# Feed-forwards' first products: 18 of 22 chunk pairs by seven half-size products each

## The chip, the cores and the metric

The kernel runs on one core of a Trainium2 chip, as one program. The metric is device microseconds (us) from its start to its end, the median of the runs shown. TensorE (PE in the profile) multiplies matrices out of SBUF into PSUM; VectorE (DVE), ScalarE (ACT) and GpSimd (POOL) work beside it on elementwise instructions, each in its own order; SyncE's queue (SP) issues most of the weight loads.

## The reference, cut to what matters

Two transformer blocks run one after the other over 512 tokens of 1024 features, in float32. Each has a gated feed-forward ahead of its token mixer and another behind it, four in all (f1, f2 in block 1, f3, f4 in block 2). Each feed-forward is

```python
DFF = 2816
u = rms_norm(x, gain)                 # (512, 1024)
a, b = jnp.split(u @ w_in, 2, axis=-1)   # w_in (1024, 5632): a the gate, b the up half
x = x + 0.5 * ((jax.nn.silu(a) * b) @ w_out)   # block 1 norms the product once more
```

The change touches `u @ w_in`, in all four places, and nothing of the mathematics behind it.

## The kernel before

Everything is held feature-major: a tile has 128 features on the partitions and the 512 tokens along it. A float32 product is made of three float32r products (`mm3`, L258 to L261): high part by high part, then the activations' low part, then the weights' low part. A weight piece is loaded as 128 x 8 x 128 floats (512 KB) into one of three `raw` buffers; ACT writes its high part (L247) and DVE the difference, its low part (L248). `lin` (L284) makes one chunk of 128 output features: 8 steps of the contraction by 3 products, 24 matmuls of 512 columns.

`ffn` (L449) goes through 22 pairs of chunks, one of the gate and one of the up half. For each pair it makes the two products (48 matmuls), multiplies both by the per-token factor R (L463 and L464, out of PSUM into SBUF on DVE), takes Silu on ACT (L94), multiplies (L466) and splits the result into high and low (L310 on ACT, L311 on DVE) for the second product with `w_out`, which follows when all 22 are there (tiles f1o, f2o, f3o, f4o). The norm's factor R comes late: the unnormalised input `g x` is split first (tiles u0 to u7), and in f1, f2 and f3 the first four chunks (pairs 0 and 1) are made ahead by `lin_ahead` (L295) in halves of 256 tokens while the stage before it still ends. f4 has nothing made ahead. Six PSUM banks of 512 columns hold chunk products at one time (NF = 6), two more the rest.

A scheduler of the language sets each engine's order of instructions from the order of the code, by its own estimate of times, and the buffers by their pools' counts. In f1, the constants of the mixers (`late_constants`, some 30 small DVE instructions, L152 to L232 and L546 to L548) are made at pair 2. Tiles of all feed-forwards lose their digits in the trace: f_3g_p is chunk 3 of the gate in whichever feed-forward the time says.

Of the kernel before, what the change touches and what calls it, by code (L numbers as in the profile page):

```python
# [18 lines left out]
P = 128  # L19
T = 512  # L20
# [8 lines left out]
FIRST = (0, DFF, P, DFF + P)  # L29
NM = 4  # L30
# [6 lines left out]
# block 1: 0-3 a step of an HGRN head, 4-7 of an mLSTM head; '.' of the products, in the order ORDER1; a-d an HGRN  # L37
# head's forget gate, e-h the silu of a convolution, A-H an output gate, w-z two gated heads; P the feed-forward's banks
# [3 lines left out]
# block 2: 0-7 a step of a stick-breaking head, a-h of a latent head; '.' and ',' of the products, in the orders ORDER2X  # L42
# and ORDER2Y; s a branch gate, q and k the scales of the latent heads
# [7 lines left out]
def block_kernel(ctx, tc, I, out):  # L51
# [3 lines left out]
    act = ctx.enter_context(tc.tile_pool(name="act", bufs=72))  # L55
    wraw = ctx.enter_context(tc.tile_pool(name="wraw", bufs=3))
# [5 lines left out]
    def psum_pools(**spec):  # L62
        """The PSUM banks shared out anew, by what they hold."""
        if "stack" in banks:
            banks["stack"].close()
        st = banks["stack"] = ExitStack()
        banks["nm"] = spec["m"]
        for tag, n in spec.items():
            banks[tag] = st.enter_context(tc.tile_pool(name="ps" + tag, bufs=n, space=PSUM, reuse_waits="tile"))
# [12 lines left out]
    def table(name):  # L82
        """The activations from here on, in this order to those before, use one table set."""
        ld = S.preload_act_table_set(name).ins  # L84
        for i in group["ins"]:
            tc.add_manual_dep(ld, i, after, reason="table")
        group["load"], group["ins"], group["name"] = ld.name, [], name
# [10 lines left out]
    def in_turn(prev, i):  # L98
        """Keeps an engine's instruction i behind the instruction named prev; the name of i."""
        if prev is not None:  # L100
            tc.add_manual_dep(i.ins, prev, after, reason="turn")
        return i.ins.name
# [74 lines left out]
    def late_constants():  # L177
# [33 lines left out]
        # the rotation's tables (cos and sin by the head norms' gains)  # L211
# [46 lines left out]
    def mm3(o, w, u, first, last):  # L258
        M.matmul(o, w[0], u[0], start=first, stop=False)  # L259
        M.matmul(o, w[0], u[1], start=False, stop=False)  # L260
        issued["last"] = M.matmul(o, w[1], u[0], start=False, stop=last).ins.name  # L261
# [3 lines left out]
    def lin_narrow(raw, n, us, R, name):  # L265
        """The product with n columns (held raw) times R, the high and low parts of the weights side by side."""
        ws = whi.tile([P, KD, 2 * n], F32R, tag="hi", name=name + "_h")
        S.activation(ws[:, :, 0:n], raw, AF.Copy)
        V.tensor_tensor(ws[:, :, n:], raw, ws[:, :, 0:n].bitcast(F32), ALU.subtract)
        o = ps(name + "_p")  # L270
        for k in range(KD):
            wide = lambda: M.matmul(o[0:2 * n, :], ws[:, k, :], us[k][0], start=k == 0, stop=k == KD - 1)
            if k == 0:
                wide()
            M.matmul(o[0:n, :], ws[:, k, 0:n], us[k][1], start=False, stop=False)
            if k > 0:
                wide()
        a, b = (A(f"{name}_{i}", shape=(n, T)) for i in range(2))
        V.tensor_tensor(a, o[0:n, :], R[0:n, :], ALU.mult)
        V.tensor_tensor(b, o[n:2 * n, :], R[n:2 * n, :], ALU.mult)  # L280
        V.tensor_tensor(a, a, b, ALU.add)
        return a

    def lin(w, c0, us, name):  # L284
        """A 128-column chunk of us^T w, feature-major."""
        if (w.tensor.name, c0) in issued:
            return issued.pop((w.tensor.name, c0))
        n = len(us)
# [30 lines left out]
    def rsqrt_newton(v, n, name):  # L319
        """1 / sqrt(v) without the activations' tables."""  # L320
# [17 lines left out]
    def token_rs(parts, n, name, blocks=range(NT), o=None, behind=None):  # L338
        """1 / sqrt(sum / n + eps) of the tokens: a square root and a step of Newton's."""
# [20 lines left out]
    class Squares:  # L360
        """The sum of the squares of the n chunks of features, as tiles to be summed over the partitions."""
# [16 lines left out]
    class Normed:  # L378
        """The parts of g x, chunk by chunk as x comes, and the per-token factor r."""
# [70 lines left out]
    def ffn(x, nx, w_in, w_out, post, nxt, ahead, name):  # L450
# [4 lines left out]
        hs = []  # L455
        for m in range(KF):
            if m == 2 and name == "f1":
                late_constants()
            n = f"{name}_{m}"
            pg = lin(w_in, m * P, us, n + "g")  # L460
            pu = lin(w_in, DFF + m * P, us, n + "u")
            gr, ur = A(n + "gr"), A(n + "ur")
            V.tensor_tensor(gr, pg, R, ALU.mult)  # L463
            V.tensor_tensor(ur, pu, R, ALU.mult)  # L464
            lut(gr, gr, AF.Silu)
            V.tensor_tensor(ur, gr, ur, ALU.mult)  # L466
            hs.append(split(ur, n + "h"))
# [11 lines left out]
    def lin_tok(w, us, c0, ncol, name, done, group=NT, bank=ps):  # L479
        """Products with the tokens on the partitions, group blocks of tokens at a time; done(t, o) takes a block's."""  # L480
# [30 lines left out]
    class Fillers:  # L511
        """Named generators, run one after the other a step at a time."""
# [17 lines left out]
    def causal_av(pd, pa, pb, v, o):  # L530
        """o[vdim, t] = sum_s v[s] p[s, t] over the blocks (diagonal, rows 0 and 2, row 1)."""
# [7 lines left out]
    def mixer1(x, nx, nxt, ahead):  # L539
# [191 lines left out]
        def mlstm_factor(hs):  # L731
            """1 / max(|den|, exp(-m)) times the head norm's factor, for the heads hs."""
# [105 lines left out]
        def head(c):  # L838
            """The next step of head c (0 to 3: HGRN, 4 to 7: mLSTM)."""
# [40 lines left out]
    def mixer2(x, nx, nxt):  # L880
# [6 lines left out]
        def sb_qk(j):  # L887
            """The queries or keys of two heads, their exact parts stacked: (high, high) against (high, low)."""
# [40 lines left out]
        def sb(h):  # L929
# [31 lines left out]
            # the parts, and those of the sums over the key blocks that follow (in place)  # L961
# [27 lines left out]
        # MLA latents  # L989
# [26 lines left out]
        def rope(src, j, t, nh, name):  # L1016
            """src (P, nh, 32), with the norm's gains of q (j=0) or k (j=1), rotated: a + b."""
# [24 lines left out]
        # queries and keys of the heads, token-major  # L1042
# [317 lines left out]
```

## Time and profile before

| what | value |
|---|---|
| runs | 2267.64, 2268.68, 2275.91 us; median 2268.68 us |
| profiled execution | its span, from the first to the last instruction, is 2267.5 us; what lies around the span is not in the trace, and the nearest run is 0.1 us above it |
| granted TensorE clock, mean | 0.993 |
| PE busy | 2247.1 us (99%) |
| DVE busy | 1151.6 us (51%) |
| ACT busy | 881.5 us (39%) |
| POOL busy | 119.6 us (5%) |

The engines work beside each other, so that their busy times don't add up. PE's busy time counts from the start of a matmul to its modelled end, and it says that PE had something in flight, not that it ran at its best rate.

### The profile page before, as it was taken

What the parts mean: (1) busy time and instruction counts of PE and PEld (TensorE: products, weight loads), DVE (VectorE), ACT (ScalarE), POOL (GpSimd) and SP (SyncE); (2) the same over time, 40 slices, a digit from 0 to 9 for tenths busy, and PEclk for the clock granted to TensorE, in tenths of its full rate; (3) what the DMA queues carried; (4) which work ended last, traced back from release to release, by engine and by line L of the source; (5) the groups of instructions that cost most, each with busy time, mean ns of one, the idle gap of its engine ahead of it and who ended that gap; (6) DMA issues with size and microseconds to landing.
All of it is one profiled execution on the core that took longest, in us unless ns stands there. A gap on an engine that the chain in (4) does not pass through costs nothing.

```text
span 2267.5 us, 27653 instructions
## 1 busy us (share of the span) xinstructions
PE 2247.1 (99%) x11074; PEld 1870.9 (83%) x11074; DVE 1151.6 (51%) x1938; ACT 881.5 (39%) x1344; POOL 119.6 (5%) x156
## 2 busy tenths in 40 slices
PE   8999999999999999999999999999999999999999
PEld 7888888888788888889888888877778888888887
DVE  5644323778648444325644433476674654444334
ACT  4323223556635333223432322566654442233222
POOL 3000001000112000001000001000000010000000
PEclk9999999999889999999999999999999999999999
DMA  5333333322112333332333333321131233333331
GB/s 151 93 96 100 95 94 91 88 62 75 38 47 85 102 93 102 93 96 73 112 93 101 89 96 104 85 66 48 46 89 34 79 112 94 102 93 96 96 107 65
DMA packets 364836, 197.22 MB, mean 87 GB/s; under 512 B 10007, under 2 KB 356516, under 8 KB 364708
## 3 DMA queue, kind: packets, MB, share of 16 engines
q1 hardware_dynamic: 364100, 195.37, 30.0%
q8 instruction: 87, 1.43, 0.3%
q0 software_dynamic: 608, 0.09, 0.0%
q14 instruction: 41, 0.34, 0.0%
HBM read 193.33 MB, written 2.10 MB: 86 GB/s over the span
## 4 chain that ended last, share of the span: by engine, by line
PE 98%; DVE 1%; ACT 0%; DMA 0%; issue 0%; SPq 0%; DVEq 0%
PE f1o_p L260 2%; PE f2o_p L259 2%; PE f2o_p L260 2%; PE f1o_p L259 2%; PE f2o_p L261 2%; PE f1o_p L261 2%; PE f4o_p L259 2%; PE f3o_p L261 2%; PE f4o_p L261 2%; PE f3o_p L259 2%; PE f3o_p L260 2%; PE f4o_p L260 2%; PE gt_p L260 1%; PE gt_p L259 1%; PE gt_p L261 1%; PE f_p L260 1%
## 5 line engine op out<-in xcount | busy, mean ns | idle before, releaser
L248 DVE TENSOR_TENSOR f1o_l<-f1o_r,f1o_h 128x1024 fp32r<-128x1024 f32 (+1 forms) x24 | 27.3, 1136 | 76.6 <-ACT f1o_h L247 76.6
L248 DVE TENSOR_TENSOR f2o_l<-f2o_r,f2o_h 128x1024 fp32r<-128x1024 f32 (+1 forms) x24 | 27.3, 1136 | 76.6 <-ACT f2o_h L247 76.6
L247 ACT ACTIVATE f2o_h<-f2o_r 128x1024 fp32r<-128x1024 f32 (+1 forms) x24 | 23.8, 990 | 85.7 <-PE f2o_p L260 73.0
L247 ACT ACTIVATE f1o_h<-f1o_r 128x1024 fp32r<-128x1024 f32 (+1 forms) x24 | 23.8, 990 | 85.7 <-PE f1o_p L260 68.4
L247 ACT ACTIVATE f3o_h<-f3o_r 128x1024 fp32r<-128x1024 f32 (+1 forms) x24 | 23.8, 990 | 85.3 <-PE f3o_p L260 53.2
L247 ACT ACTIVATE f4o_h<-f4o_r 128x1024 fp32r<-128x1024 f32 (+1 forms) x24 | 23.8, 990 | 85.0 <-PE f4o_p L260 52.8
L376 POOL TENSOR_TENSOR f_acc<-f_acc,f_sq 128x256 f32<-128x256 f32 (+1 forms) x42 | 38.9, 927 | 316.9 <-ACT f_sq L375 299.5
L248 DVE TENSOR_TENSOR f3o_l<-f3o_r,f3o_h 128x1024 fp32r<-128x1024 f32 (+1 forms) x24 | 27.3, 1136 | 54.0 <-ACT f3o_h L247 54.0
L248 DVE TENSOR_TENSOR f4o_l<-f4o_r,f4o_h 128x1024 fp32r<-128x1024 f32 (+1 forms) x24 | 27.3, 1135 | 52.5 <-ACT f4o_h L247 52.5
L84 ACT ACT_TABLE_LOAD x36 | 46.2, 1283 | 1.4 <-PEq L1341 0.8
L376 POOL TENSOR_TENSOR m_acc<-m_acc,m_sq 128x256 f32<-128x256 f32 (+1 forms) x18 | 20.1, 1115 | 348.8 <-ACT m_sq L375 348.8
L260 PE MATMUL m1o_p<-mix_l,m1o_h 128*128 128x256 f32 (+1 forms) x88 | 29.3, 334 | 0.0
L261 PE MATMUL m1o_p<-mix_h,m1o_l 128*128 128x256 f32 (+1 forms) x88 | 29.2, 334 | 0.0
L259 PE MATMUL m1o_p<-mix_h,m1o_h 128*128 128x256 f32 (+1 forms) x88 | 28.6, 336 | 0.0
L376 POOL TENSOR_TENSOR pl_acc<-pl_acc,pl_sq 128x512 f32<-128x512 f32 x6 | 10.3, 1710 | 341.6 <-ACT pl_sq L375 341.6
L248 DVE TENSOR_TENSOR gt_l<-gt_r,gt_h 128x1024 fp32r<-128x1024 f32 x16 | 19.6, 1224 | 12.9 <-ACT gt_h L247 12.6
L94 ACT ACTIVATE l<-l 128x384 f32<-128x384 f32 (+1 forms) x48 | 24.2, 554 | 3.1 <-DVE l L949 3.0
L247 ACT ACTIVATE pg_h<-pg_r 128x1024 fp32r<-128x1024 f32 x8 | 8.5, 1061 | 42.6 <-PE pp L496 19.4
L94 ACT ACTIVATE e<-ms,mx,sck 128x512 f32<-128x512 f32 (+3 forms) x32 | 19.5, 614 | 14.0 <-DVE mx L1135 13.8
L260 PE MATMUL wo_p<-mg_l,wo_h 128*128 128x512 f32 x64 | 24.8, 390 | 0.0
L259 PE MATMUL wo_p<-mg_h,wo_h 128*128 128x512 f32 x64 | 24.8, 389 | 0.0
L376 POOL TENSOR_TENSOR f2p_acc<-f2p_acc,f2p_sq 128x512 f32<-128x512 f32 x6 | 7.7, 1288 | 322.9 <-ACT f2p_sq L375 322.9
(4287 smaller groups left out, 7533.5 us busy)
## 6 DMA issues: line engine op xcount, KB each, us to landing
f1o_r<-in_ffn_w_out_dram SPq DMA_DIRECT2D x16, 512.0 KB, 3.8
f2o_r<-in_ffn_w_out_dram SPq DMA_DIRECT2D x16, 512.0 KB, 4.3
f3o_r<-in_ffn_w_out_dram SPq DMA_DIRECT2D x16, 512.0 KB, 4.3
gt_r<-in_w_in_dram SPq DMA_DIRECT2D x16, 512.0 KB, 4.0
f4o_r<-in_ffn_w_out_dram SPq DMA_DIRECT2D x16, 512.0 KB, 4.1
f_r<-in_ffn_w_in_dram SPq DMA_DIRECT2D x12, 512.0 KB, 5.0
mg_r<-in_w_mix_in_dram SPq DMA_DIRECT2D x8, 512.0 KB, 4.0
m1o_r<-in_w_mix_out_dram SPq DMA_DIRECT2D x8, 512.0 KB, 4.2
```

Of the source, the lines that this page charges most:

```text
L84: ld = S.preload_act_table_set(name).ins
L94: i = S.activation(out, in_, func, **kw).ins
L247: S.activation(hi, raw, AF.Copy)
L248: V.tensor_tensor(lo, raw, hi.bitcast(F32), ALU.subtract)
L259: M.matmul(o, w[0], u[0], start=first, stop=False)
L260: M.matmul(o, w[0], u[1], start=False, stop=False)
L261: issued["last"] = M.matmul(o, w[1], u[0], start=False, stop=last).ins.name
L376: G.tensor_tensor(acc[:, sl], acc[:, sl], q[:, sl], ALU.add)
```

## The change

Pairs 4 to 21 of each feed-forward (18 of 22) are made in another way. Gate chunk, up chunk, the two halves of the 1024 features and the two halves of the 512 tokens make a 2 x 2 by 2 x 2 block product, and Strassen's scheme (in Winograd's form) makes it of seven block products in place of eight, with sums and differences of the blocks ahead and behind. A block product here has 4 steps of the contraction by 3 products: 12 matmuls of 256 columns; seven of them are 84. Two of them share an accumulator, so that four regions of 256 columns (`ab`, `cd`, two banks) hold a pair.

`strassen_input` runs once per feed-forward: it makes the normalised input `un = g x R` (8 DVE instructions of 512 columns), 16 differences of 256 columns on POOL, and 28 forms of 256 columns, each split into a high part (ACT) and a low part (DVE). Evictions of pairs 0 and 1 are written between its parts. `strassen_pair` loads the two weight chunks (`r0`, `r1`), makes four sums of 512 columns on POOL, and splits four weight matrices a, b, c and d (1024, 512, 1024 and 1024 columns; in before two of 1024). Its evictions are two ACT copies and five DVE instructions of 256 columns that read PSUM (and mostly one SBUF tile). The steps of a pair and of the next are written interleaved. The splits of all 22 results stand behind the last pair, `late_constants` at pair 6. There are 70 activation buffers for 72, and 4 raw buffers for 3. Comments and docstrings went too. The core of the diff:

```diff
+NDIRECT = 4
+HT = T // 2
+HK = KD // 2
...
-    act = ctx.enter_context(tc.tile_pool(name="act", bufs=72))
-    wraw = ctx.enter_context(tc.tile_pool(name="wraw", bufs=3))
+    act = ctx.enter_context(tc.tile_pool(name="act", bufs=70))
+    wraw = ctx.enter_context(tc.tile_pool(name="wraw", bufs=4))
...
+    def strassen_input(x, nx, R, between):
+        un, forms = [None] * KD, [{} for _ in range(HK)]
+        def normed(k):
+            un[k] = A(f"{nx.name}_n{k}")
+            V.scalar_tensor_tensor(un[k], x[k], nx.g(k), R, ALU.mult, ALU.mult)
+        def form(k, name, src, sign=1.0):
+            t = A(f"{nx.name}_{name}{k}", F32R)
+            hi, lo = t[:, 0:HT], t[:, HT:]
+            S.activation(hi, src, AF.Copy, scale=sign)
+            if sign > 0:
+                V.tensor_tensor(lo, src, hi.bitcast(F32), ALU.subtract)
+            else:
+                V.scalar_tensor_tensor(lo, src, sign, hi.bitcast(F32), ALU.mult, ALU.subtract)
+            forms[k][name] = hi, lo
+        for k in range(HK):
+            normed(k)
+            form(k, "b11", un[k][:, 0:HT])
+        between(0)
+        for k in range(HK):
+            normed(HK + k)
+            form(k, "b21", un[HK + k][:, 0:HT])
+        between(1)
+        d1, d2 = [], []
+        for k in range(HK):
+            b11, b12, b22 = un[k][:, 0:HT], un[k][:, HT:], un[HK + k][:, HT:]
+            d1.append(A(f"{nx.name}_d1{k}"))
+            G.tensor_tensor(d1[k][:, 0:HT], b12, b11, ALU.subtract)
+            G.tensor_tensor(d1[k][:, HT:], b22, b12, ALU.subtract)
+            form(k, "n1", d1[k][:, 0:HT], -1.0)
+        for k in range(HK):
+            form(k, "t3", d1[k][:, HT:])
+        for k in range(HK):
+            b21, b22 = un[HK + k][:, 0:HT], un[HK + k][:, HT:]
+            d2.append(A(f"{nx.name}_d2{k}"))
+            G.tensor_tensor(d2[k][:, 0:HT], b22, d1[k][:, 0:HT], ALU.subtract)
+            G.tensor_tensor(d2[k][:, HT:], d2[k][:, 0:HT], b21, ALU.subtract)
+            form(k, "t2", d2[k][:, 0:HT], -1.0)
+        for k in range(HK):
+            form(k, "b22", un[HK + k][:, HT:])
+            form(k, "t4", d2[k][:, HT:])
+        return forms
+    def strassen_pair(w, c0, c1, forms, name, done):
+        r0, r1 = (wraw.tile([P, KD, P], F32, tag="raw", name=f"{name}_r{i}") for i in range(2))
+        for r, c in ((r0, c0), (r1, c1)):
+            nc.sync.dma_start(out=r, in_=w[:, c:c + P].rearrange("(k p) c -> p k c", p=P))
+        def parts(r, nm, n=KD):
+            if n == KD:
+                hi, lo = whi.tile([P, n, P], F32R, tag="hi", name=nm + "_h"), wlo.tile([P, n, P], F32R, tag="lo",
+                                                                                     name=nm + "_l")
+            else:
+                hi, lo = (act.tile([P, n, P], F32R, tag="a", name=f"{nm}_{j}") for j in "hl")
+            S.activation(hi, r, AF.Copy)
+            V.tensor_tensor(lo, r, hi.bitcast(F32), ALU.subtract)
+            return [(hi[:, k, :], lo[:, k, :]) for k in range(n)]
+        first, last = slice(0, HK), slice(HK, KD)
+        g1 = parts(r0, name + "a")
+        s1 = act.tile([P, HK, P], F32, tag="a", name=name + "_s1")
+        G.tensor_tensor(s1, r1[:, first], r1[:, last], ALU.add)
+        g2 = parts(s1, name + "b", HK)
+        G.tensor_tensor(r1[:, first], r0[:, first], r1[:, first], ALU.add)
+        g3 = parts(r1, name + "c")
+        G.tensor_tensor(r0[:, first], r0[:, first], s1, ALU.add)
+        G.tensor_tensor(r0[:, last], r0[:, last], r0[:, first], ALU.add)
+        g4 = parts(r0, name + "d")
+        def product(o, ws, form, start, stop, more=False):
+            for k in range(HK):
+                mm3(o, ws[k], forms[k][form], start and k == 0, stop and k == HK - 1, more)
+        ab, cd = ps(name + "_ab"), ps(name + "_cd")
+        (a, b), (c, d) = ((t[:, 0:HT], t[:, HT:]) for t in (ab, cd))
+        sab, o1, o2 = A(name + "_s"), A(name + "_o1"), A(name + "_o2")
+        product(a, g1[:HK], "b11", True, False)
+        product(b, g1[HK:], "b21", False, True)
+        yield
+        S.activation(sab[:, HT:], b, AF.Copy)
+        V.tensor_tensor(o1[:, 0:HT], a, sab[:, HT:], ALU.add)
+        product(c, g2, "n1", True, False)
+        product(d, g3[:HK], "t3", False, True)
+        product(a, g4[:HK], "t2", False, True, True)
+        S.activation(sab[:, 0:HT], a, AF.Copy)
+        V.tensor_tensor(o2[:, HT:], c, sab[:, 0:HT], ALU.add)
+        V.scalar_tensor_tensor(o2[:, HT:], o2[:, HT:], -1.0, d, ALU.mult, ALU.subtract)
+        yield
+        product(c, g4[HK:], "b22", False, False, True)
+        product(d, g3[HK:], "t4", False, True, True)
+        V.tensor_tensor(o1[:, HT:], c, sab[:, 0:HT], ALU.add)
+        V.scalar_tensor_tensor(o2[:, 0:HT], d, -1.0, sab[:, 0:HT], ALU.mult, ALU.subtract)
+        done(o1, o2)
+        yield
     def ffn(x, nx, w_in, w_out, post, nxt, ahead, name):
         if banks["nm"] != NF:
             psum_pools(m=NF, x=8 - NF)
         us, R, _ = nx.factor()
         table("silu_and_others")
-        hs = []
-        for m in range(KF):
-            if m == 2 and name == "f1":
-                late_constants()
+        hs = [None] * KF
+        def direct(m):
             n = f"{name}_{m}"
-            pg = lin(w_in, m * P, us, n + "g")
-            pu = lin(w_in, DFF + m * P, us, n + "u")
-            gr, ur = A(n + "gr"), A(n + "ur")
+            return lin(w_in, m * P, us, n + "g"), lin(w_in, DFF + m * P, us, n + "u")
+        def gated(m, gr, ur):
+            lut(gr, gr, AF.Silu)
+            V.tensor_tensor(ur, gr, ur, ALU.mult)
+            hs[m] = ur
+        def evict(m, pg, pu):
+            gr, ur = A(f"{name}_{m}gr"), A(f"{name}_{m}ur")
             V.tensor_tensor(gr, pg, R, ALU.mult)
             V.tensor_tensor(ur, pu, R, ALU.mult)
-            lut(gr, gr, AF.Silu)
-            V.tensor_tensor(ur, gr, ur, ALU.mult)
-            hs.append(split(ur, n + "h"))
+            gated(m, gr, ur)
+        ready = [direct(m) for m in range(2)]
+        forms = strassen_input(x, nx, R, lambda i: evict(i, *ready[i]))
+        for m in range(2, NDIRECT):
+            evict(m, *direct(m))
+        pairs = {m: strassen_pair(w_in, m * P, DFF + m * P, forms, f"{name}_{m}",
+                                  lambda gr, ur, m=m: gated(m, gr, ur)) for m in range(NDIRECT, KF)}
+        run(pairs[NDIRECT], 1)
+        for m in range(NDIRECT, KF):
+            if m == NDIRECT + 2 and name == "f1":
+                late_constants()
+            run(pairs[m], 1)
+            if m + 1 < KF:
+                run(pairs[m + 1], 1)
+            run(pairs[m])
+        hs = [split(hs[m], f"{name}_{m}h") for m in range(KF)]
...
```

On DVE, at the start of f2 (names are f2's; R is the per-token factor, n0 to n7 the normalised input, b11 and the like the low parts of the forms, gr and ur the evicted chunk products), stood before:

```order
L393 COPY f2_R_6031<-f2_sp_6032 128x512
L463 TENSOR_TENSOR f2_0gr_6039<-f2_0_p_5705,f2_R_6031 128x512
L464 TENSOR_TENSOR f2_0ur_6040<-f2_2816_p_5706,f2_R_6031 128x512
L466 TENSOR_TENSOR f2_0ur_6040<-f2_0gr_6039,f2_0ur_6040 128x512
L248 TENSOR_TENSOR f2_4u_0_l_6237<-f2_4u_0_r_6234,f2_4u_0_h_6236 128x1024
```

and there stands now, at the same place:

```order
L396 COPY f2_R_7145<-f2_sp_7146 128x512
L466 SCALAR_TENSOR_TENSOR f2_n0_7153<-x0_156,pcola_117,f2_R_7145 128x512
L466 SCALAR_TENSOR_TENSOR f2_n1_7158<-x1_157,pcola_117,f2_R_7145 128x512
L473 TENSOR_TENSOR f2_b110_7155<-f2_n0_7153,f2_b110_7155 128x256
L466 SCALAR_TENSOR_TENSOR f2_n2_7163<-x2_158,pcola_117,f2_R_7145 128x512
L473 TENSOR_TENSOR f2_b111_7160<-f2_n1_7158,f2_b111_7160 128x256
L466 SCALAR_TENSOR_TENSOR f2_n3_7168<-x3_159,pcola_117,f2_R_7145 128x512
L473 TENSOR_TENSOR f2_b112_7165<-f2_n2_7163,f2_b112_7165 128x256
L578 TENSOR_TENSOR f2_0gr_7173<-f2_0_p_6819,f2_R_7145 128x512
L579 TENSOR_TENSOR f2_0ur_7174<-f2_2816_p_6820,f2_R_7145 128x512
```

The first eviction of a PSUM bank (0gr) was next behind R and is now eighth behind it. The low part of the second weight matrix of the first Strassen pair (4b_l) stands on DVE at the end of the whole input stage:

```order
L473 TENSOR_TENSOR f2_t42_7280<-f2_d22_7253,f2_t42_7280 128x256
L473 TENSOR_TENSOR f2_b223_7283<-f2_n7_7194,f2_b223_7283 128x256
L473 TENSOR_TENSOR f2_t43_7286<-f2_d23_7259,f2_t43_7286 128x256
L573 TENSOR_TENSOR f2_2ur_7352<-f2_2gr_7351,f2_2ur_7352 128x512
L519 TENSOR_TENSOR f2_4b_l_7436<-f2_4_s1_7433,f2_4b_h_7435 128x512
```

From n0 up to and with 4b_l there are 48 instructions, 20 of 512 and 28 of 256 columns; before, DVE had nothing of this kind. On PE, at the end of f2's first products (h are the split results, 21_ab and 21_cd the banks of the last pair), products of the second matrix stand between the last two steps of pair 21:

```order
L264 MATMUL f2_21_ab_9513<-f2_t23_7262,f2_21d_l_9510 128x256
L262 MATMUL f2o0_p_9748<-f2_0h_h_9639,f2o0_0_h_9732 128x512
L263 MATMUL f2o0_p_9748<-f2_0h_l_9640,f2o0_0_h_9732 128x512
L264 MATMUL f2o0_p_9748<-f2_0h_h_9639,f2o0_0_l_9733 128x512
L262 MATMUL f2o0_p_9748<-f2_1h_h_9643,f2o0_0_h_9732 128x512
L263 MATMUL f2o0_p_9748<-f2_1h_l_9644,f2o0_0_h_9732 128x512
L264 MATMUL f2o0_p_9748<-f2_1h_h_9643,f2o0_0_l_9733 128x512
L262 MATMUL f2o0_p_9748<-f2_2h_h_9647,f2o0_0_h_9732 128x512
L262 MATMUL f2_21_cd_9514<-f2_b220_7265,f2_21d_h_9509 128x256
```

Before, each result was split in its own turn of the loop; now the 22 splits stand behind the last pair in the code, and the first of them is waited for here.

## Rows read from the trace of the kernel before

**Rows 1.** The page: the engines, and the chain that ended last.

```profile
PE 2247.1 (99%) x11074; PEld 1870.9 (83%) x11074; DVE 1151.6 (51%) x1938; ACT 881.5 (39%) x1344; POOL 119.6 (5%) x156
...
PE 98%; DVE 1%; ACT 0%; DMA 0%; issue 0%; SPq 0%; DVEq 0%
```

**Rows 2.** Timeline of PE in f2 (start us, us, engine, line, operation, out<-in).

```profile
726.75 0.39 PE L259 MATMUL f_3g_p<-f_u0h,f_3g_h 128*128 128x512 f32 x1
...
737.63 0.39 PE L259 MATMUL f_4g_p<-f_u0h,f_4g_h 128*128 128x512 f32 x1
...
933.47 0.39 PE L259 MATMUL f2o_p<-f_0h_h,f2o_h 128*128 128x512 f32 x1
```

**Rows 3.** Chain of waits, chunks made ahead in halves, one step of 12 matmuls each.

```profile
704.53 0.48 PE f_p L259 x4
705.97 0.48 PE f_p L259 x4
...
711.73 0.48 PE f_p L259 x4
```

**Rows 4.** Timeline of DVE at the start of f2.

```profile
724.81 0.69 DVE L393 COPY f_R<-f_sp 128x512 f32<-128x512 f32 x1
725.60 0.69 DVE L463 TENSOR_TENSOR f_0gr<-f_p,f_R 128x512 f32<-128x512 f32 x1
...
727.94 1.23 DVE L248 TENSOR_TENSOR f_4u_l<-f_4u_r,f_4u_h 128x1024 fp32r<-128x1024 f32 x1 [0.26 <-ACT f_4u_h L247]
729.08 0.68 DVE L311 TENSOR_TENSOR f_0h_l<-f_0ur,f_0h_h 128x512 fp32r<-128x512 f32 x1
729.68 0.68 DVE L463 TENSOR_TENSOR f_1gr<-f_p,f_R 128x512 f32<-128x512 f32 x1
```

**Rows 5.** Timeline of DVE, instructions of 256 columns, POOL idle.

```profile
699.67 0.48 DVE L314 SCALAR_TENSOR_TENSOR f_u7l<-x,pcola,f_u7h 128x256 fp32r<-128x256 f32 x1 [0.18 <-ACT f_u7h L313]
...
700.52 0.42 DVE L440 TENSOR_TENSOR x<-x,m_y 128x256 f32<-128x256 f32 x1
700.87 0.42 DVE L439 TENSOR_TENSOR m_y<-m_y,m1p 128x256 f32<-128x256 f32 x1
```

**Rows 6.** Timeline of DVE and POOL, each beside the other, both reading SBUF.

```profile
702.67 0.86 POOL L376 TENSOR_TENSOR f_acc<-f_acc,f_sq 128x256 f32<-128x256 f32 x1 [3.85 <-ACT f_sq L375]
702.85 0.96 DVE L314 SCALAR_TENSOR_TENSOR f_u1l<-x,pcola,f_u1h 128x256 fp32r<-128x256 f32 x1
...
703.92 0.74 POOL L376 TENSOR_TENSOR f_acc<-f_acc,f_sq 128x256 f32<-128x256 f32 x1 [0.40 <-ACT f_sq L375]
...
664.73 1.29 POOL L376 TENSOR_TENSOR m1p_acc<-m1p_acc,m1p_sq 128x512 f32<-128x512 f32 x1 [37.12 <-ACT m1p_sq L375]
665.63 1.47 DVE L248 TENSOR_TENSOR m1o_l<-m1o_r,m1o_h 128x1024 fp32r<-128x1024 f32 x1 [0.79 <-ACT m1o_h L247]
666.80 2.82 POOL L376 TENSOR_TENSOR m1p_acc<-m1p_acc,m1p_sq 128x512 f32<-128x512 f32 x2 [0.78 <-ACT m1p_sq L375]
668.70 2.00 DVE L248 TENSOR_TENSOR m1o_l<-m1o_r,m1o_h 128x1024 fp32r<-128x1024 f32 x1 [1.60 <-ACT m1o_h L247]
```

**Rows 7.** Timeline of POOL and DVE in mixer 1, DVE with a PSUM input (sb).

```profile
615.06 1.00 POOL L784 TENSOR_TENSOR ws<-wd,wa 128x384 f32<-128x384 f32 x1 [0.45 <-DVE wa L780]
...
615.64 0.42 DVE L781 SCALAR_TENSOR_TENSOR wb<-sb,wb 128x256 f32<-128x256 f32 x1 [0.66 <-PE sb L778]
```

**Rows 8.** Timeline of DVE and PE in f1, around the late constants.

```profile
73.74 0.28 DVE L186 TENSOR_TENSOR ix<-ix,ix 128x128 int32<-128x128 int32 x1
...
84.94 1.23 DVE L248 TENSOR_TENSOR f_7g_l<-f_7g_r,f_7g_h 128x1024 fp32r<-128x1024 f32 x1 [0.37 <-ACT f_7g_h L247]
...
78.25 0.47 PE L259 MATMUL f_5g_p<-f_u0h,f_5g_h 128*128 128x512 f32 x1 [1.38 <-DVE f_2gr L463]
```

**Rows 9.** Timeline in f4 of DVE and PE: R, and chunk 4 of the gate.

```profile
1853.63 0.69 DVE L393 COPY f_R<-f_sp 128x512 f32<-128x512 f32 x1 [2.34 <-PE f_sp L357]
...
1885.67 0.39 PE L259 MATMUL f_4g_p<-f_u0h,f_4g_h 128*128 128x512 f32 x1
```

**Rows 10.** Timeline of ACT at the start of f2.

```profile
726.86 1.04 ACT L247 ACTIVATE f_4u_h<-f_4u_r 128x1024 fp32r<-128x1024 f32 x1
727.81 0.62 ACT L310 ACTIVATE f_0h_h<-f_0ur 128x512 fp32r<-128x512 f32 x1
```

**Rows 11.** List of DMA issues in f2 (count, KB each, median us to landing).

```profile
f_10u_r<-in_ffn_w_in_dram SPq DMA_DIRECT2D x1, 512.0 KB, 4.2
```

More of the change, by code (lines that the diff above doesn't have):

```diff
@@ L256, in wcols, with mm3 @@
         return r
[L258 to L261, printed above, removed]
+    def mm3(o, w, u, first, last, more=False):
+        M.matmul(o, w[0], u[0], start=first, stop=False, skip_group_check=more)
+        M.matmul(o, w[0], u[1], start=False, stop=False, skip_group_check=more)
+        issued["last"] = M.matmul(o, w[1], u[0], start=False, stop=last, skip_group_check=more).ins.name
     issued = {}
```

## The prediction, made before the result was known

> **What bounds the kernel now.** I read the page first: PE is busy for 99% of the span and makes 98% of the chain that ended last, while DVE works for half of it and POOL for a twentieth [rows 1]. So time can only be won by giving PE less to do, and DVE, ACT and POOL have idle time to give, as long as PE never waits for them. Then I read PE's timeline in f2. Chunk 3 of the gate starts at 726.75 and chunk 4 at 737.63 [rows 2], so a pair of 48 matmuls of 512 columns takes 10.88 us, 226.7 ns each. From there to the first product with the second matrix, at 933.47 [rows 2], lie 206.72 us, or 19 pairs (3 to 21) of 10.88: PE never waits in the whole stage. The four stages together hold 72 pairs that the change touches. Third, I read how DVE and POOL stand to each other where both work, since the change gives both of them much to do at one time.
>
> **The gain on PE.** A new pair is 84 matmuls of 256 columns. Such matmuls are in the trace where four chunks are made ahead in halves: steps of 12 start at 704.53, 705.97 and 711.73 [rows 3], five steps in 7.20 us, 120 ns for each matmul, each with a weight load of its own, as they will have here. So a pair takes 84 x 0.120 = 10.08 us in place of 10.88. It has an eighth fewer columns, but each column at 256 costs more (0.469 ns for 0.443), and of the 12.5% only 7.4% are left: 0.80 us a pair, 57.6 us for 72. This is the whole gain, 2.5% of the span.
>
> **The cost in the steady state.** Per pair DVE has three lo parts of 1024 columns, issued 1.14 us apart (727.94 to 729.08), two instructions of 512 with both inputs in SBUF, 0.60 apart [rows 4], and five evictions of 256, 0.35 apart [rows 5]: 3.42 + 1.20 + 1.75 = 6.4 us. ACT has three of 1024 at 1.04, one of 512 and one Silu at 0.62 [rows 10] and two short copies, about 5.2 us. POOL has four sums of 512 at 1.29 [rows 6], 5.2 us. Each is under 10.08. But DVE and POOL hinder each other. DVE's instruction at 702.85 took 0.96 us where the same one alone takes 0.48 [rows 5], with POOL at work in the first 0.68 of it; the one at 668.70 took 2.00 where 1.23 is usual [rows 4], with POOL at work until 669.62, for 0.92 of it; the one at 665.63 took 1.47, with POOL until 666.02, for 0.39 of it [rows 6]. It lost 0.48 of 0.68, 0.77 of 0.92 and 0.24 of 0.39: about 0.7 of the time in which POOL ran. With an input in PSUM it lost nothing: 0.42 us at 615.64, all of it beside POOL [rows 7], as alone. So of DVE's time in a pair, 4.6 us can be held up, by 0.7 x 5.2 = 3.6: DVE then has 6.4 + 3.6 = 10.0 us of 10.08 if every POOL instruction meets such work of DVE's, and less where POOL runs beside evictions or DVE's idle time. This is close. Because the weights are prepared one pair ahead, I take it to be just hidden, 0 a pair; the upper bound, if DVE and POOL trail each other, is +0.8 (a pair as slow as before). The loads (two of 512 KB a pair, 4.2 us each [rows 11], four buffers) are hidden.
>
> **The cost at the start of f1, f2 and f3.** I work it out for f2 and take it three times, since f1 and f3 have the same order. DVE can begin n0 where 0gr stood, at 725.60 [rows 4]. PE's next chunk, 3 of the gate, needs a PSUM bank that 0gr frees; PE wants it at 726.75 [rows 2]. Now 0gr is the eighth from n0 on: four of 512 and three of 256 ahead and its own 0.68 make 4.1 us, and one or two POOL differences hold DVE 0.5 us each (below): PE goes on at about 730.2, 3.5 us late (3.0 without POOL). Next PE has pair 3 directly, 10.88 us, and the first step of pair 4, 24 matmuls or 2.88 us, and stands at 744.0 before the product with matrix b. That needs 4b_l, the 48th instruction from n0. Without POOL: 20 x 0.60 + 28 x 0.35 = 21.8 us. On POOL 16 differences at 0.74 and one sum at 1.29 [rows 6] must lie ahead of it; at 0.7 they hold DVE for 8.3 + 0.9 = 9.2 us. So 4b_l is ready at 725.6 + 31.0 = 756.6: PE waits 12.6 us. Matrices c and d follow with 0.6 us more. Together 16.7 us for a stage, **50 us** for the three. The bounds: with no hindrance 4b_l is ready at 747.4 and PE wants it at 743.5, so 6.9 us a stage, 21 in all; with each POOL instruction holding DVE for its full length (13.1 us for 9.2) 20.6 a stage, 62 in all. I take 0.7, since three pairs of rows show it.
>
> Here a rule speaks against the change. The Trainium skill, in "SBUF — State Buffer", section "Who interferes with whom", states that a DVE instruction with two SBUF inputs contends with a GpSimd instruction that reads SBUF, that DVE with one SBUF input does not, and that the second to issue fully blocks until the first ends. The rows agree on which instructions are hit (0.42 us beside POOL with a PSUM input [rows 7]), and show 0.6 to 0.85 of the overlap lost [rows 6] in place of all of it. By the rows the sum is the one below; by the rule the starts cost 62 us.
>
> f4 has no chunk made ahead, so PE has four direct pairs: R is there at 1853.63 and chunk 4 of the gate starts at 1885.67 [rows 9]. 1854.3 + 31.0 = 1885.3 is ahead of the step after next, at 1888.6: under 1 us is left, counted as 0.8.
>
> **The end of each first product.** The scheduler set seven products of the second matrix ahead of the last step of pair 21, and they need splits that used to be made long before. After the last matmul of the step before, ACT has an eviction of 256 and a split of 512 (0.4 and 0.62 [rows 10]), then DVE a split of 0.68 [rows 4], of which two or three matmuls' time is covered: some 1.6 us of wait, four times 6.4 us. Below, 0 if ACT runs the split early; above, 4 each. All 22 splits (13.2 us of DVE) then run beside 17.9 us of PE work; that fits barely.
>
> **The late constants.** From 73.74 to 84.94 [rows 8], 11.2 us, DVE made them between seven instructions of 512 and a lo part (5.3 us): 5.9 us, and PE waited 1.4 for it. At pair 6 DVE has no such room: 5.9 in place of 1.4, +4.5 us (0 to 8).
>
> **Sum.** 2267.5 - 57.6 + 50.1 + 0.8 + 6.4 + 4.5 = 2271.7 us, against a median of 2268.7 of the runs shown, 1.2 us above the profiled span. A measurement of this kernel tells about 0.5%, 11 us, from no change; so the forecast is no change, **2272 us**: three stalls at the starts give back what 72 pairs win.
>
> **The rivals.**
> *The starts are mostly covered.* If the scheduler's order leaves POOL running beside the evictions (PSUM inputs) and DVE's idle time, the starts cost 21 us, the ends and constants perhaps 5: 2267.5 - 57.6 + 26 = 2236, faster. For it speaks that DVE is not held with a PSUM input [rows 7]; against it, that in those 48 instructions only eight read PSUM. It decides from a stall of 12 us a stage downwards. 2230 to 2257; chance 0.25.
> *Full blocking.* Each POOL instruction stops DVE for its whole length: 3 x 3.9 = 12 more, 2284, slower. For it: 0.77 lost of 0.92; against: 0.24 of 0.39 [rows 6]. The rule named above is this rival. 2280 to 2290; chance 0.13.
> *DVE and POOL bound the steady state.* 6.4 us of DVE and 5.2 of POOL that exclude each other but for the evictions (1.75) come to 9.8 to 11.6 us. From 10.08 on PE waits in every pair, and at 10.88 nothing is won at all: +0.5 to +0.8 on 72 pairs, 36 to 58 us, so 2308 to 2330, slower. For it: 10.0 of 10.08 by my own factor; against: the weights are prepared a pair ahead. Chance 0.15.
> *The change doesn't do what it says.* If matmuls of 256 columns take 126 ns here (two accumulators in one bank, forms in new tiles), a pair takes 10.6 and 36 us of the gain are missing: 2308. Against it, the 60 matmuls of [rows 3] kept 120 ns over changing weights and banks. Chance 0.05.
>
> **How the numbers follow.** The forecast keeps 0.42 (own range 2258 to 2281). Faster by over 0.5%: the first rival and a little of the forecast's lower edge, 0.27. Within 0.5%: 0.41. Slower: 0.32, from the other three and the upper edge. The range leaves out the lowest tenth (the covered starts at their best) and the highest (a steady state at break-even): 2238 to 2306.
>
> **What would show it.** In f2, PE's pairs 5 to 20 should start 10.08 us apart with no wait on a lo part (L519); at 10.5 or more the third rival holds. The list of waits should show PE waiting for 0gr (L578) some 3.5 us and for 4b_l some 12 us in f1, f2 and f3; DVE's lo parts beside POOL should be longer than 1.23. PE should wait for f_0h at each stage's end for 1 to 3 us. What would make it wrong: waits of under 6 us at the starts (faster), a pair over 10.3 us (slower), or a granted clock that falls in those long waits of PE, which I count at nothing.

## The result, and the profile after

The changed kernel takes 2305.09 us (median; 2302.92 to 2310.6) against 2268.61 us for the kernel before, a ratio of 1.0154 with a 95% interval of 1.0129 to 1.018: slower by 1.5%. The profiled execution took 2310.6 us with a span of 2308.9, 41.4 us above the span before. The forecast was 2272 with a range of 2238 to 2306: the time lies just inside the range's upper edge, and the case called likeliest, no change, is not what came. That it lies inside is luck in part: that side of the range stood for full blocking and for a slower steady state, and neither made the time.

The page of the changed kernel (engines; granted clock in 40 slices, in tenths; the chain that ended last):

```profile
PE 2218.8 (96%) x13666; PEld 1968.1 (85%) x13666; DVE 1499.7 (65%) x2442; ACT 1060.9 (46%) x1744; POOL 608.2 (26%) x508
...
PEclk9899999999979799999989999999999999999999
...
PE 90%; DVE 7%; issue 1%; POOL 1%; ACT 1%; DMA 0%; SPq 0%; DVEq 0%; ACTq 0%; POOLq 0%
```

Beside [rows 1], PE has 28 us less to do and yet holds only 90% of the chain; 7% of it have gone to DVE. The clock falls in three slices that stood at 9 before, at the starts of f1, f2 and f3 (the fourth low one, in mixer 1, was low before too). The list of PE's waits says at what (engine, line, waits for; us in total, times, longest):

```profile
PE f_cd L262 <- ACT f_4b_h L518: 35.9, 4, 11.1
PE f_cd L264 <- DVE f_4b_l L519: 12.7, 4, 3.4
PE f_3g_p L262 <- DVE f_0gr L578: 10.8, 3, 4.3
...
PE f_ab L264 <- DVE f_7a_l L519: 4.3, 1, 4.3
PE f_cd L262 <- DVE f_o L550: 1.9, 1, 1.9
```

Four stages wait for matrix b of the first Strassen pair, three for the first eviction, one for the constants. Outside of the starts, the first steps of pairs 10, 11 and 19 of f2 stand in PE's timeline so:

```profile
841.25 0.28 PE L262 MATMUL f_ab<-f_b,f_10a_h 128*128 128x256 f32 x1
...
851.33 0.28 PE L262 MATMUL f_ab<-f_b,f_11a_h 128*128 128x256 f32 x1
...
931.97 0.28 PE L262 MATMUL f_ab<-f_b,f_19a_h 128*128 128x256 f32 x1
```

10.08 us from pair to pair, with no wait, to the hundredth what [rows 3] gave. So the gain on PE is all there, 57.6 us, and everything else lies at the edges of the stages. What the starts of PE's matmuls in the four stages give, each distance against the one that the matmuls in it take without a wait: 11.5 us from chunk 2 to chunk 3, 10.88 for a direct pair, and 0.12 us for each matmul of 256. Between the first matmuls of pairs 4 and 5 lie 38 of these and between those of 5 and 6 lie 96 (in f4 50 and 84), since the scheduler lets a pair's first matmuls run ahead of the steps before; for the same reason 94 lie between pair 21's first matmul and the first product with the second matrix, not the 84 of a pair.

| what | predicted, us | measured, us (f1, f2, f3, f4) |
|---|---|---|
| 72 pairs | -57.6 | -57.6 |
| wait for the first eviction | 10.5 | 11.3 (3.4, 4.5, 3.4, 0) |
| wait for matrix b and what follows it | 39.6 and 0.8 | 43.8 (14.9, 14.0, 14.9) and 6.6 in f4 |
| slower matmuls behind these waits | 0 | 15.3 (4.1, 5.3, 4.1, 1.8) |
| ends of the first products | 6.4 | 7.2 (1.8 each) |
| constants in f1 | 4.5 | 9.2 |
| mixers and the rest | 0 | 5.6 |
| sum | +4.2 | +41.4 |

**The start of f2.** DVE and POOL in the stretch before 4b_l (timeline; POOL's L525 to L530 are the sums of weights of pairs 4 and 5, DVE's L475 the low parts of t2):

```profile
749.65 1.41 DVE L466 SCALAR_TENSOR_TENSOR f_n<-x,pcola,f_R 128x512 f32<-128x512 f32 x2
...
762.46 0.93 POOL L491 TENSOR_TENSOR f_d<-f_n,f_n 128x256 f32<-128x256 f32 x1
762.71 0.68 DVE L578 TENSOR_TENSOR f_1gr<-f_p,f_R 128x512 f32<-128x512 f32 x1
...
770.46 1.47 POOL L525 TENSOR_TENSOR f_s<-f_r 128x512 f32<-128x512 f32 x1
772.01 1.32 POOL L527 TENSOR_TENSOR f_r<-f_r,f_r 128x512 f32<-128x512 f32 x1
773.41 1.33 POOL L529 TENSOR_TENSOR f_r<-f_r,f_s 128x512 f32<-128x512 f32 x1
774.82 1.32 POOL L530 TENSOR_TENSOR f_r<-f_r 128x512 f32<-128x512 f32 x1
...
777.62 1.32 POOL L527 TENSOR_TENSOR f_r<-f_r,f_r 128x512 f32<-128x512 f32 x1
...
773.54 5.68 DVE L475 SCALAR_TENSOR_TENSOR f_t<-f_d,f_t 128x256 fp32r<-128x256 f32 x4
779.14 0.41 DVE L473 TENSOR_TENSOR f_b<-f_n,f_b 128x256 fp32r<-128x256 f32 x1
...
784.82 0.68 DVE L519 TENSOR_TENSOR f_4b_l<-f_s,f_4b_h 128x512 fp32r<-128x512 f32 x1
```

While POOL does its six sums in a row, DVE gets one instruction through per sum: four of 256 columns take 5.68 us, 1.4 us each, as long as a POOL sum, where the next one, with POOL done, takes 0.41. POOL itself is hardly slowed in these sums (mostly 1.32 for 1.29). The eviction 1gr, which reads PSUM, takes its usual 0.68 us although POOL works beside it. And ACT cannot make 4b_h any sooner, although its input s1 is there at 772:

```profile
772.13 0.40 ACT L471 ACTIVATE f_t<-f_d 128x256 fp32r<-128x256 f32 x1
780.19 0.63 ACT L97 ACTIVATE f_2gr<-f_2gr 128x512 f32<-128x512 f32 x1 [7.66 <-DVE f_2gr L578]
780.73 0.61 ACT L518 ACTIVATE f_4b_h<-f_s 128x512 fp32r<-128x512 f32 x1
```

On ACT it is queued behind the Silu of chunk 2, which waits 7.66 us for an eviction on DVE, which stands behind the held forms. So the list names ACT for the most part of the wait, and DVE's queue is what is late.

**The clock.** Windows of f2 (columns as [rows 1]'s engines in us busy and count, then granted clock, DMA share, GB/s):

```profile
744.00:750.00 6.00, 6.00 (x30) 4.92 (x29) 2.27 (x3) 1.06 (x1) 0.00 (x0) 1.00 0.84 211
750.00:755.00 5.00, 0.69 (x3) 0.36 (x2) 5.00 (x9) 2.11 (x5) 1.10 (x1) 0.83 0.00 2
755.00:760.00 5.00, 5.00 (x13) 3.84 (x13) 5.00 (x8) 1.12 (x4) 4.14 (x4) 0.50 0.01 2
760.00:765.00 5.00, 5.00 (x23) 4.16 (x22) 5.00 (x7) 2.64 (x8) 4.92 (x7) 0.99 0.00 0
...
775.00:780.00 5.00, 0.00 (x0) 0.00 (x0) 5.00 (x6) 0.00 (x0) 3.86 (x3) 0.50 0.00 0
...
785.00:790.00 5.00, 4.45 (x21) 4.45 (x22) 4.84 (x6) 0.12 (x1) 0.03 (x1) 0.50 0.29 84
790.00:795.00 5.00, 5.00 (x40) 5.00 (x40) 1.44 (x3) 0.90 (x2) 2.92 (x3) 0.91 0.46 129
```

After PE's wait of 4.3 us the clock is at 0.50, 1.2 GHz, for five microseconds in which PE has work (x13 against x23 in the next window), and again after the long wait. In f4, too, it is at 0.50 behind the waits for matrix b (from 1942 to 1944.5). The low clock while PE stands idle costs nothing; that behind it does. In PE's timeline matmuls of 256 columns then start 0.21 us apart, not 0.12:

```profile
785.93 0.42 PE L262 MATMUL f_cd<-f_n,f_4b_h 128*128 128x256 f32 x1
786.15 0.42 PE L263 MATMUL f_cd<-f_n,f_4b_h 128*128 128x256 f32 x1
...
791.22 0.29 PE L262 MATMUL f_ab<-f_t,f_4d_h 128*128 128x256 f32 x1
791.34 0.28 PE L263 MATMUL f_ab<-f_t,f_4d_h 128*128 128x256 f32 x1
```

**The end of f2.** ACT, and the first second product on PE:

```profile
963.61 0.38 ACT L548 ACTIVATE f_s<-f_ab 128x256 f32<-128x256 f32 x1 [2.27 <-PE f_ab L264]
963.89 0.62 ACT L313 ACTIVATE f_0h_h<-f_0ur 128x512 fp32r<-128x512 f32 x1
...
964.56 0.50 PE L262 MATMUL f2o_p<-f_0h_h,f2o_h 128*128 128x512 f32 x1 [0.99 <-ACT f_0h_h L313]
```

ACT is idle for 2.27 us with the split of result 0 behind an eviction that waits for PE; then PE waits for the split.

### The profile page after: what moved, and what is told of

Its sections match the earlier page's. It is cut to its first block, busy times and chain, and to the rows that moved or that the text cites. A ratio compares the mean times of both kernels' runs of the same rounds, so it can differ in the third digit from the quotient of the medians.

```text
span 2308.9 us, 34318 instructions
## 1 busy us (share of the span) xinstructions
PE 2218.8 (96%) x13666; PEld 1968.1 (85%) x13666; DVE 1499.7 (65%) x2442; ACT 1060.9 (46%) x1744; POOL 608.2 (26%) x508
## 4 chain that ended last, share of the span: by engine, by line
PE 90%; DVE 7%; issue 1%; POOL 1%; ACT 1%; DMA 0%; SPq 0%; DVEq 0%; ACTq 0%; POOLq 0%
PE f_cd L264 6%; PE f_cd L262 6%; PE f_cd L263 6%; PE f_ab L263 4%; PE f_ab L262 4%; PE f_ab L264 4%; PE f1o_p L263 2%; PE f3o_p L263 2%; PE f4o_p L263 2%; PE f2o_p L263 2%; PE f1o_p L264 2%; PE f1o_p L262 2%; PE f4o_p L264 2%; PE f3o_p L264 2%; PE f2o_p L264 2%; PE f4o_p L262 2%
## 5 line engine op out<-in xcount | busy, mean ns | idle before, releaser
L529 POOL TENSOR_TENSOR f_r<-f_r,f_s 128x512 f32<-128x512 f32 x72 | 112.9, 1568 | 268.1 <-issue 44.0
L548 ACT ACTIVATE f_s<-f_ab 128x256 f32<-128x256 f32 x72 | 27.6, 384 | 240.3 <-PE f_ab L264 240.2
L527 POOL TENSOR_TENSOR f_r<-f_r,f_r 128x512 f32<-128x512 f32 x72 | 118.0, 1640 | 5.6
L525 POOL TENSOR_TENSOR f_s<-f_r 128x512 f32<-128x512 f32 x72 | 98.9, 1374 | 43.1 <-DMA f_r<-in_ffn_w_in_dram 41.4
L530 POOL TENSOR_TENSOR f_r<-f_r 128x512 f32<-128x512 f32 x72 | 93.7, 1301 | 5.6
L543 ACT ACTIVATE f_s<-f_ab 128x256 f32<-128x256 f32 x72 | 27.5, 382 | 114.6 <-PE f_ab L264 114.6
L549 DVE TENSOR_TENSOR f_o<-f_cd,f_s 128x256 f32<-128x256 f32 x72 | 30.6, 424 | 76.1 <-ACT f_s L548 76.1
L97 ACT ACTIVATE f_o<-f_o 128x512 f32<-128x512 f32 x72 | 45.5, 632 | 29.0 <-DVE f_o L554 25.6
L544 DVE TENSOR_TENSOR f_o<-f_ab,f_s 128x256 f32<-128x256 f32 x72 | 30.5, 424 | 42.2 <-ACT f_s L543 42.2
L573 DVE TENSOR_TENSOR f_o<-f_o,f_o 128x512 f32<-128x512 f32 x72 | 48.9, 679 | 0.4 <-ACT f_o L97 0.4
```

The lines of the kernel that those rows point to most:

```text
L525: G.tensor_tensor(s1, r1[:, first], r1[:, last], ALU.add)
L527: G.tensor_tensor(r1[:, first], r0[:, first], r1[:, first], ALU.add)
L529: G.tensor_tensor(r0[:, first], r0[:, first], s1, ALU.add)
L530: G.tensor_tensor(r0[:, last], r0[:, last], r0[:, first], ALU.add)
```

## The experiments

Each is the changed kernel with one edit, the last three a combination. Runs 1 to 6 were timed once each, against 2302.92 to 2310.6 us for the changed kernel; the kernel before ranged from 2264.55 to 2276.37 in the runs beside them. A difference of some 10 us is therefore read from the stages of the trace and not from the time alone: each from chunk 2 to its last second product, the four stages together took 1356.0 us before, 1391.9 in the changed kernel, and 1366.2, 1371.2, 1349.2, 1394.8, 1382.6 and 1395.1 in runs 1 to 6.

**1 and 2. POOL's sums moved to DVE**, all of them, and those of the weights alone:

```diff
-            G.tensor_tensor(d1[k][:, 0:HT], b12, b11, ALU.subtract)
+            V.tensor_tensor(d1[k][:, 0:HT], b12, b11, ALU.subtract)
...
-        G.tensor_tensor(s1, r1[:, first], r1[:, last], ALU.add)
+        V.tensor_tensor(s1, r1[:, first], r1[:, last], ALU.add)
```

> All sums of the change (16 of the input in each feed-forward, 4 of weights in each pair) stand on DVE, none on POOL. Theory A (a DVE instruction with two SBUF inputs and a POOL tensor_tensor go one at a time, so POOL's work is added to DVE's at each start): the stretch from n0 to the low part 4b_l, 35.9 us in f2 in the changed kernel (749.65 to 785.5), loses the holds and gains 16 x 0.35 and some 6 x 0.60 us on DVE, 21.8 + 5.6 + 3.6 = 31 us; PE's wait for matrix b of pair 4 falls from about 13 to 8 us in f1, f2 and f3 and from 7 to 3 in f4, and the run is at about 2285 us. Theory B (DVE's own 48 instructions and their order make the stretch, POOL beside them costs little): the stretch grows by 9 us to 45, and the run is at about 2335. Both expect pairs of 10.08 us in the steady state, since DVE then has 8.8 us a pair.

> Only the sums of weights (4 a pair) move from POOL to DVE, the 16 of the input stay. Theory A: in f2 six sums of pairs 4 and 5 ran on POOL before 4b_l and let DVE through with one instruction each, 8.4 us of POOL; on DVE they cost 3.6 us, so the stretch from n0 to 4b_l falls from 35.9 to about 32 and the run to about 2290. Theory B: the stretch grows by 3.6 us, run about 2320. Pairs in the steady state 10.08 us by both.

Measured: 2278.89 us without POOL, 2293.26 with the weight sums alone on DVE. The stretch from n0 to the end of 4b_l in f2 fell from 35.85 us to 29.14 and 31.23. DVE's rows at its two ends, of the first run and then of the second:

```profile
737.29 1.42 DVE L466 SCALAR_TENSOR_TENSOR f_n<-x,pcola,f_R 128x512 f32<-128x512 f32 x2
...
765.75 0.67 DVE L519 TENSOR_TENSOR f_4b_l<-f_s,f_4b_h 128x512 fp32r<-128x512 f32 x1
...
747.16 1.42 DVE L466 SCALAR_TENSOR_TENSOR f_n<-x,pcola,f_R 128x512 f32<-128x512 f32 x2
...
777.72 0.67 DVE L519 TENSOR_TENSOR f_4b_l<-f_s,f_4b_h 128x512 fp32r<-128x512 f32 x1
```

DVE was given more work and was done sooner: theory A. PE's waits in f2 without POOL (as in the list above, for this stretch alone):

```profile
PE f_cd L262 <- ACT f_4b_h L518: 3.8, 1, 3.8
PE f_3g_p L262 <- DVE f_0gr L578: 3.8, 1, 3.8
PE f_cd L264 <- DVE f_4b_l L519: 3.2, 1, 3.2
```

7.0 us for matrix b where it was 13.5. The stretches of the two runs give POOL's price too. Without POOL, DVE has 16 instructions of 256 and three of 512 more ahead of 4b_l (the differences, two sums of weights and the product 3ur): 23 x 0.60 + 44 x 0.35 = 29.2 us, and 29.14 were measured, so that nothing holds DVE there. With all 22 POOL instructions before 4b_l the stretch is 14.1 us over DVE's own 21.8. With the 16 differences alone on POOL it is 9.4 over, of which 1.8 are the three instructions of 512; so the 16 hold DVE for 7.6 us, 0.48 each, and the six sums of 512 for the other 6.4, 1.1 each. In the steady state DVE is busy for 8.7 of 10 us without POOL (800 to 810), and a pair is still 10.08 us.

**3. Six direct pairs in place of four.**

```diff
-NDIRECT = 4
+NDIRECT = 6
```

> Six pairs of each feed-forward are direct and 16 by seven products (4 and 18 in the changed kernel); nothing else is changed. If PE lacks work while DVE prepares (theory C), two more direct pairs, 21.8 us, cover the stretch: the waits for matrix b of the first Strassen pair go (about 13 us in f1, f2 and f3, 7 in f4) and with them about 2.5 us each of lowered clock behind them; a wait of some 4 us for a PSUM bank takes their place in f1 to f3, because pair 2 is still evicted behind all forms; 8 pairs fewer give back 6.4 us. Run about 2268. The rival: DVE has as much more to do for the direct pairs (3.5 us each) and orders it ahead, so that the wait only moves: 2290 to 2300.

Measured: 2271.08 us, 34 less. PE's waits in f2 are now

```profile
PE f_3g_p L262 <- DVE f_0gr L578: 5.4, 1, 5.4
...
PE f_cd L264 <- DVE f_6c_l L519: 0.8, 1, 0.8
```

The wait for matrix b is gone in all four stages, as theory C has it. The wait for a bank at pair 5 did not come: DVE evicts 2gr at 768.90, and PE comes to chunk 5 at 772.15. DVE's stretch is longer (43.2 us, with the direct pairs' own instructions in it), and that costs nothing under PE's work.

**4. Evictions of pairs 0 and 1 ahead of the forms.**

```diff
-        forms = strassen_input(x, nx, R, lambda i: evict(i, *ready[i]))
+        for i in range(2):
+            evict(i, *ready[i])
+        forms = strassen_input(x, nx, R, lambda i: None)
```

> Pairs 0 and 1 are evicted ahead of the input's forms, as in the kernel before, instead of between them. If the stretch up to 4b_l alone sets when PE goes on (theory C), the waits for 0gr at the start of f1 to f3 (3.4 to 4.5 us) go but the wait for matrix b grows by as much, and the run stays at 2300 to 2306, less some 5 us where the clock no longer falls behind the first wait. If the two waits are independent, the run is 18 us shorter, 2287.

Measured: 2308.39 us, no gain. In f2 the wait for the first eviction is gone, and

```profile
PE f_cd L262 <- ACT f_4b_h L518: 15.2, 1, 15.2
PE f_cd L264 <- DVE f_4b_l L519: 3.4, 1, 3.4
```

18.6 us where the two waits before were 17.8 together. The two are one debt: while DVE's stretch ends late, it does not matter where PE stands waiting. In f4, which had no first eviction to wait for, the edit only costs: the waits for matrix b grow from 3.6 and 2.6 us to 7.1 and 3.3.

**5. The constants behind the last pair.**

```diff
-            if m == NDIRECT + 2 and name == "f1":
-                late_constants()
...
         hs = [split(hs[m], f"{name}_{m}h") for m in range(KF)]
+        if name == "f1":
+            late_constants()
```

> The mixers' constants of f1 are made behind the last pair's splits, beside the second products, in place of pair 6; nothing else is changed. The forecast's step on the constants, in its corrected size: the step from pair 7 to pair 8 in f1 falls from 20.95 us to 10.08 and 2 us elsewhere in f1 go too, the run is 11 to 13 us shorter than the changed kernel, about 2294. Rival: DVE is as short of time behind the last pair (22 splits wait there), so that the second products wait 5 to 8 us for splits: 2300.

Measured: 2295.28 us. From pair 7 to pair 8 it is 10.08 us again, and f1, from chunk 2 to the first second product, is 10.5 us shorter (224.95 for 235.50); from there to the last one it takes 0.15 us more (125.20 for 125.05). The rival's waits behind the last pair don't come.

**6. Four splits early.**

```diff
                 run(pairs[m + 1], 1)
+            if m + 2 == KF:
+                early = [split(hs[i], f"{name}_{i}h") for i in range(4)]
             run(pairs[m])
-        hs = [split(hs[m], f"{name}_{m}h") for m in range(KF)]
+        hs = early + [split(hs[m], f"{name}_{m}h") for m in range(4, KF)]
```

> The first 4 of the 22 results of each feed-forward are split one step earlier, before the last half of pair 20 and the rest of pair 21. If the end of each first product waits for these splits, its loss of 3.0 us (2.35 ahead of the first product with the second matrix and 0.66 within) falls to under 1 in all four: 2297. Rival: DVE and ACT have no room there, the last pairs' own low parts come late instead, and the time stays at 2303 to 2308.

Measured: 2313.8 us, no gain; neither expectation quite. PE's waits at the end of f2:

```profile
PE f2o_p L262 <- ACT f_4h_h L313: 1.0, 1, 1.0
PE f2o_p L264 <- DVE f2o_l L251: 1.0, 1, 1.0
```

The wait of 1.0 us for result 0 became one for result 4, the first that is not yet split, since the scheduler put as many more second products ahead of the last step of pair 21; another 1.0 us for the weights' low part came to it. So what makes PE wait is the order of ACT behind the eviction, not how many splits stand there. There was also less to win than the expectation's 3.0 us an end: it counts 84 matmuls where 94 stand, and the loss is 1.8 us in the changed kernel, 2.7 here.

**7 to 9. Combinations.** Six direct pairs, constants last, and evictions of pairs 0 and 1 next behind R, of pair 2 between the forms:

```diff
-        ready = [direct(m) for m in range(2)]
-        forms = strassen_input(x, nx, R, lambda i: evict(i, *ready[i]))
-        for m in range(2, NDIRECT):
+        ready = [direct(m) for m in range(3)]
+        for i in range(2):
+            evict(i, *ready[i])
+        forms = strassen_input(x, nx, R, lambda i: evict(2, *ready[2]) if i else None)
+        for m in range(3, NDIRECT):
```

Run 7 has four splits early and the sums on POOL, run 8 the sums on DVE, run 9 is run 8 with all splits late.

> Six direct pairs, evictions of pairs 0 and 1 next behind R and of pair 2 between the forms, four splits early, constants last; the sums stay on POOL. Gain of 64 pairs 51.2 us. Theory A: PE reaches matrix b of pair 6 some 36 us behind n0, while the preparation takes about 40 with POOL's holds, so f1 to f3 still wait some 4 us each, plus 2 us each of lowered clock; ends 1 us each: 2268.6 - 51.2 + 18 + 4 + 3 = about 2242. Theory B (POOL costs nothing once PE is covered): 2225.

> The same, with all sums on DVE. Theory A: the preparation takes about 32 us and lies wholly under the direct pairs; no wait in f1 to f4 over 1 us, granted clock as in the kernel before, pairs of 10.08 us: about 2225, faster than the kernel before by 1.9%. Theory B: DVE has 28% more to do than with POOL's help and PE waits for it: 2245 or more, slower than the version with POOL.

> The combined version with all sums on DVE, but all 22 splits behind the last pair again. By the runs before this one, four early splits made the end of each first product worse, not better (from the start of pair 21's first step to the last second product of f2 138.4 to 139.1 us with them, 137.5 without): if that holds in the combined version the run is 4 x 1.0 to 1.6 us shorter than with them, 2234 to 2237. Rival (the difference there came from where POOL stood): the same time, 2241.

Measured: 2255.38 us with POOL (ratio to the kernel before 0.993, interval 0.9913 to 0.9947), 2240.8 without (0.987, 0.9847 to 0.9893), and 2232.61 with late splits (0.9822, 0.9798 to 0.9845). Runs 7 and 8 are 13 and 16 us above what theory A forecast (2242, 2225), run 9 just under its 2234 to 2237. Half of run 8's miss is the harm of the early splits, 8.2 us to run 9, which is more than run 6 showed of it; the other half, and run 7's miss, were not traced. B is refuted for both, since the version without POOL is the faster by 15 us. The longest waits of PE in f2 in run 9, the version that beats both kernels by 1.8% and 3.1%:

```profile
PE f2o_p L262 <- ACT f_0h_h L313: 1.0, 1, 1.0
PE f_cd L264 <- DVE f_6b_l L519: 0.6, 1, 0.6
PE f_ab L262 <- ACT f_7a_h L518: 0.4, 1, 0.4
```

Its mean granted clock is 0.994, that of the kernel before 0.993.

## Why the prediction was right and wrong

*The gain* (10.08 us a pair, 57.6 in all) is right to the hundredth, and with it that the steady state hides DVE, ACT, POOL and the loads. The rival that DVE and POOL bound the steady state is refuted, by the trace and, with all of POOL's work on DVE, by run 1.

*The waits at the starts* are right in place and nearly in size: 55.1 us in f1 to f3 for 50.1. That it comes so near is luck in part, since two errors work against each other. The stretch from n0 to 4b_l was forecast as 31.0 us and measured as 35.85; what I mis-sized is the count of POOL instructions ahead of 4b_l. I counted one sum of weights, and POOL, whose sums wait for nothing of DVE's there, did six. The hold of a POOL instruction, 0.7 of its length, is right on the whole: 14.1 us for the 19.6 that the 22 instructions take alone, 0.72 (0.48 of 0.74 us for the short ones and 1.1 of 1.29 for the long ones); with six sums the same working gives 21.8 + 8.3 + 5.4 = 35.5. On the other side PE came to its wait later than forecast, by 1.0 us of the first wait and 2.7 of slow matmuls (f2).

The rule of the Trainium skill ("SBUF — State Buffer", "Who interferes with whom"), that the two engines' shared port pair is an exclusive lock, agrees with the traces after in what it does to DVE: a DVE instruction of 256 columns takes 1.4 us beside a POOL sum of 1.32 and 0.41 alone. It does not agree for the whole: with strict turns the sums would start 1.29 + 0.35 = 1.64 us apart and they start 1.40 apart, and over the stretch 14.1 us were lost, not 19.6, in part because some of POOL's work stood beside evictions out of PSUM, as 1gr above, which lost nothing. For a plan the measured 0.72 decides.

*The clock* is the step that was left out: "counted at nothing". It cost 15.3 us at the four starts, 1.7 to 2.7 behind each first wait and behind each wait for matrix b, at half speed; the text named it only as what could make the prediction wrong. That it hangs on the waits is seen where they are gone: in run 4 the chunk behind the removed first wait takes 5.44 us again, where it took 8.10, and in run 9 the mean clock is back at its old value.

*f4* was taken with the stretch of f2, 31.0 us; there DVE also has the low parts of direct chunks between the forms, and the stretch is 40.3 us: 6.6 us of wait in place of 0.8, and 1.8 of slow matmuls behind it.

*The ends* were right in mechanism and size, 1.6 us forecast for the eviction and split that PE waits for and 1.8 measured. The waits that the list names make 1.2 of it, as [0.99 <-ACT] above.

*The constants* were sized by what DVE spent on them before (5.9 us); at pair 6 they cost 11.0 (4.3 and 1.9 as named waits; the clock is low there too), 9.2 more than before. Run 5 shows that all of it goes when they are moved.

*The rest*, 5.6 us, lies almost wholly between the stages. Mixer 1, from the last second product of f1 to the first product of its output, took 255.0 us before, 258.5 in the changed kernel and 251.1 to 261.4 in the experiments, none of which edits it. Its time goes with the granted clock: the mean clock of this stretch is 0.94 before, 0.93 in the changed kernel, 0.96 where it took 251.1 and 0.92 where it took 261.4. Whether a version or the run makes the clock differ there was not tried.

So the sum failed by 37 us: clock 15.3, f4 5.8, rest 5.6, starts 5.0, constants 4.7 and ends 0.8. The forecast of no change needed the sum within 11 of nothing. The largest step that failed is the clock, put at nothing although the forecast itself had three waits of 12 us; after it come DVE's stretch, too short in all four stages, and the constants.

## What to carry to other kernels

A scheme that saves a few per cent in the steady state of a dense TensorE loop is worth it only if its preparation lies under other TensorE work: here 57.6 us were won exactly as counted, and 93 lost at the stages' edges and on the constants, until two more direct pairs covered the preparation, the sums stood on DVE and the constants had moved (run 9). Work that moves from a half idle DVE to an idle POOL is no relief when both read two SBUF inputs: count each POOL instruction as time taken from DVE (0.72 of its length here), and count all that POOL will run by then, not those that the path needs. A wait of TensorE of three or more microseconds cost more than its length here, since the clock fell behind it.

## What the runs showed of the hardware that was not expected

DVE and POOL take turns one instruction for one where both have work with SBUF inputs: a short DVE instruction with two SBUF inputs (0.41 us alone) lasts as long as the POOL sum beside it (1.4 for 1.32 us). POOL's sums of 512 pay almost nothing for it (mostly 1.32 for 1.29); its differences of 256 in the same stretch took 0.74 to 1.45 us, 0.99 in the mean, for 0.74. With POOL's sums moved onto DVE, 7.4 us more for it to do ahead of 4b_l (16 x 0.35 and three of 0.60), its stretch became 6.7 us shorter. And after a TensorE wait of 3.3 to 4.3 us the granted clock fell to 0.50, in f2 before the work came back and in f1 and f3 some 1.4 us after it, for 1.7 to 2.7 us of loss.
